# Down's column chunks taken in pairs with seven block products in two K pairs of each part, and token forms kept per K pair

## The chip, the core and the metric

The kernel runs on one core of a Trainium2 chip. The metric is the device time in microseconds (us) of one execution of the whole program. The median of three runs of the kernel before is 2602.59 us (2600.7 to 2604.3). Names of engines: TensorE (PE, and PEld for its weight loads), VectorE (DVE), ScalarE (ACT), GpSimd (POOL), and SyncE (SP), which issues the DMAs.

## The reference

A decoder trunk of two layers runs over 256 tokens of width 2048 in float32. Layer 0 has a state-space mixer, layer 1 differential attention, and each is followed by a SwiGLU FFN of width 5632. Every sub-layer has a norm ahead of it and one behind it:

```python
for i in range(DEPTH):
    h = rmsnorm(x, norm_mix_pre[i])
    m = ssd_mixer(h, ...) if i % 2 == 0 else diff_attention(h, ...)
    x = x + rmsnorm(m, norm_mix_post[i])
    h = rmsnorm(x, norm_ffn_pre[i])
    m = (silu(h @ ffn_w_gate[i]) * (h @ ffn_w_up[i])) @ ffn_w_down[i]
    x = x + rmsnorm(m, norm_ffn_post[i])
```

"Down" in this document is the product with `ffn_w_down` (5632 x 2048), "gate" and "up" those with the other two (2048 x 5632 each).

## The kernel before

**Products.** A float32 matrix product is made from two parts of each operand, hi (the value rounded to the type fp32r) and lo (the rest), as three matmuls: hi by hi, hi by lo, lo by hi. A matmul has a 128 x 128 block of activations as the stationary operand (128 rows of K, 128 tokens) and a 128 x 512 block of weights as the moving one. The 256 tokens are two halves, t = 0 and 1. A **K pair** is 256 rows of K (two blocks j), a **column chunk** is 512 output columns.

**Feeding.** Weights are loaded as 128 x 2048 tiles `raw` (1 MB) in a pool of three buffers; SP issues the loads in program order. `prep` (L112) then makes hi with a ScalarE cast (L119) and lo with a VectorE subtraction (L120), in a pool of four buffers each. If a split is late, TensorE waits. Weights that are split once serve both token halves.

**`mv` (L159)** is the plain product: for one column chunk it runs over K pairs. In each one it does t = 0 at once, puts t = 1 on the list `pending`, where it stays for `lag` K pairs, and calls `tick`. The two sums lie in PSUM (pool `accp`, four buffers), and `evac` is called for t when the last K pair of that t is done.

**`pair` (L201)** takes two column chunks at once, so that one K pair is a 2 x 2 x 2 product (token half, j, column chunk) of eight blocks, 24 matmuls. In the K pairs named by `SEVEN = (3, 5)` it takes seven block products, 21 matmuls, in the manner of Strassen and Winograd. That needs four sums of weight blocks (VectorE, L239 to L242), a second split of these sums, and four **token forms**, sums and differences of activation blocks, as stationary operands. Its order within such a K pair is: three products that need no sums of weights (p1, (0,0), (0,1), nine matmuls), a `tick`, then p6, p5, p7 and (1,0), which need the sums. p1, p5, p6, p7 are collected over both K pairs in their own PSUM tiles (pool `auxp`, four buffers, which the transposes of activations use as well). After the last seven-product K pair a ScalarE copy (L256) and four VectorE combinations (L257 to L260) make four tiles of them in SBUF, which `done` adds when a sum is complete. Gate and up of column chunks 0 to 9 go this way, the last chunk, 10, goes through `mv`.

**The FFN.** `ffn` (L699) runs gate and up in three parts of column chunks, (10, 0, 1), (2, 3, 4, 5), (6, 7, 8, 9), and behind each part does Down over the K pairs which that part has produced: 6, 8 and 8 K pairs. So Down of a part begins right behind the up pair that yields its last activations. `u_done` (L748) makes silu(gate) x up with two VectorE operations for each of four 128 x 512 pieces (L752, L753); `act_piece` transposes a piece on TensorE (L271) and splits it (L264, L265). The transposes are put off by two steps with `later(2, piece)`. `later`, `tick` and `lookup` are a list of deferred work: `tick` runs what is due, `lookup` runs it at once if something is needed.

**Down.** `out_proj` (L594) calls `mv` for n = 0 to 3, the four column chunks of the output, over the K pairs `kgs` of the part. The tiles m[(t, n)] hold the sum over parts: part one copies PSUM to them (L608), the others add (L610). In the last part, m[(t, n)] also enters the row's sum of squares, and is multiplied by the weights of the post-norm, `wpost`, one row of 512 columns that a DMA spreads over 128 partitions (L673). This product is made on GpSimd for n = 0, 1, 2 and on VectorE for n = 3 (L600). `load_post` keeps one n at a time in one buffer: when another n is asked for, it is loaded into the same buffer. After n = 3 follows `norm_chain` (L566), which completes the norm, adds the residual `x` and transposes it (`ptx`, L574) for the next sub-layer.

**Buffers for forms and for x.** `make_forms` (L717) makes the forms of a block of two K pairs, hence four token forms for each, though only one of the two K pairs is in `SEVEN`. It stores hi and lo in tiles with the tag `xr`, four buffers. The residual x, written to DRAM (`xr_d`) at the start of the FFN, is read back into tiles of the same tag by `fetch_x` (L688) ahead of the last part's Down.

**Order.** The program text gives dependencies; a scheduler then orders the instructions on each engine, as far as they allow. So the place of an instruction in an engine's queue isn't that of the text.

Of the kernel before, what the change touches and what calls it, by code (L numbers as in the profile page):

```python
# [30 lines left out]
LAG2 = 2  # L31

SEVEN = (3, 5)


@with_exitstack
def trunk_kernel(ctx, tc, x_rows, x_cols, vec_cols, vec64, post_rows, lam_rows,
# [110 lines left out]
    def lookup(dct, key):  # L148
        while key not in dct:
            deferred.popleft()[1]()  # L150
        return dct[key]
# [46 lines left out]
                    evac(ct, acc[ct][:, :S], acc[ct][:, S:])  # L198
            tick()

    def pair(blocks, seven, form, done):  # L201

        flush()
        acc = {}  # L210
        end = len(blocks) - 1

        def mm(k, st, hi, lo, last):
            first = k not in acc
            if first:
                acc[k] = (auxp.tile([P, 512], F32, tag="aux", name="cp") if isinstance(k, str) else
                          accp.tile([P, 512], F32, tag="acc", name="acc"))
            for q, (a, b) in enumerate(((st[0], hi), (st[0], lo), (st[1], hi))):
                nc.tensor.matmul(acc[k], a, b, start=first and q == 0, stop=last and q == 2)  # L219

        ss = {}
        for kp, src in enumerate(blocks):
            raw = rawp.tile([P, 4, 512], F32, tag="raw", name="raw")
            for c in range(2):
                nc.sync.dma_start(raw[:, 2 * c:2 * c + 2], src[c])
            if kp not in seven:
                hi, lo = prep(raw)
                for t in range(NT):
                    for c, e in ((0, 2), (1, 0)):
                        for j in range(2):  # L230
                            mm((t, c), x_stat(2 * kp + j, t), hi[:, e + j], lo[:, e + j], kp == end and j == 1)
                        if kp == end:
                            done(t, c, acc[(t, c)], ss)
                    tick()
                continue
            last = kp == seven[-1]
            hi, lo = prep(raw[:, 1:4])

            nc.vector.tensor_tensor(raw[:, 2], raw[:, 2], raw[:, 0], op=ALU.add)  # L239
            nc.vector.tensor_tensor(raw[:, 0], raw[:, 0], raw[:, 1], op=ALU.add)  # L240
            nc.vector.tensor_tensor(raw[:, 1], raw[:, 1], raw[:, 2], op=ALU.add)
            nc.vector.tensor_tensor(raw[:, 3], raw[:, 3], raw[:, 1], op=ALU.add)  # L242
            sh, sl = prep(raw)
            k0, k1 = 2 * kp, 2 * kp + 1
            mm("p1", x_stat(k0, 0), hi[:, 1], lo[:, 1], last)
            mm((0, 0), x_stat(k1, 0), hi[:, 2], lo[:, 2], False)
            mm((0, 1), form(kp, 3), hi[:, 0], lo[:, 0], False)
            tick()
            mm("p6", form(kp, 2), sh[:, 1], sl[:, 1], last)
            mm("p5", form(kp, 0), sh[:, 2], sl[:, 2], last)  # L250
            mm("p7", form(kp, 1), sh[:, 0], sl[:, 0], last)
            mm((1, 0), x_stat(k1, 1), sh[:, 3], sl[:, 3], False)
# [338 lines left out]
        if not final:  # L591
            later(2, stats)

    def out_proj(w, first, last, acts, kgs, step, final, lag, t512, pw, scale=None, ns=range(4)):  # L594

        def sums(t, n):
            mt = m[(t, n)]
            row_sumsq(ss4[t][:, n:n + 1], mt, t512("junk"))
            dst = t512("mw") if n == 3 else mt
            (nc.vector if n == 3 else nc.gpsimd).tensor_tensor(dst, mt, pw(n), op=ALU.mult)  # L600
            return dst

        ss4 = {}
        for n in ns:
            def evac(t, ps, n=n):
                if first:
                    m[(t, n)] = mpool.tile([P, 512], F32, tag="m", name="m")
                    nc.scalar.copy(m[(t, n)], ps)  # L608
                else:
                    nc.vector.tensor_tensor(m[(t, n)], m[(t, n)], ps, op=ALU.add)  # L610
                if not last:
                    return
                if t not in ss4:
                    ss4[t] = small.tile([P, 4], F32, tag="ss4", name="ss_m", bufs=3)
                    for e in range(n):
                        sums(t, e)
                dst = sums(t, n)
                if n == 2:
                    p3 = small.tile([P, 1], F32, tag="ss1", name="p3", bufs=3)
                    nc.vector.tensor_reduce(p3, ss4[t][:, 0:3], axis=AX.X, op=ALU.add)  # L620
                    nc.vector.tensor_scalar(ss4[t][:, 0:1], p3, 1.0 / D, EPS, op0=ALU.mult, op1=ALU.add)
                if n == 3:
                    norm_chain(t, ss4[t], dst, step, final, t512)

            def stat(i, j, t):
                hi, lo = lookup(acts, (t, kgs[i] // 2))
                jj = (kgs[i] % 2) * 2 + j
                return hi[:, jj], lo[:, jj]
# [49 lines left out]

    def xr_tile(name):
        return postp.tile([P, 2, 512], F32, tag="xr", name=name, bufs=4)

    def fetch_x(src):
        for t in range(NT):
            for h in range(2):
                xt = xr_tile("x")
# [14 lines left out]
    def ffn(wg, wu, wd, step, final):  # L702
# [14 lines left out]
        def make_forms(n):  # L717

            xf = []
            for t in range(NT):  # L720
                xf.append(t512("xf", (P, 4, P)))
                sl = slice(t * P, (t + 1) * P)
                nc.vector.tensor_tensor(xf[t], xT_hi[n][:, :, sl].bitcast(F32), xT_lo[n][:, :, sl].bitcast(F32), op=ALU.add)
            fa, fb = (t512("f", (P, 2, 2, P)) for _ in range(2))
            nc.vector.tensor_tensor(fa[:, 0], xf[1][:, 0:4:2], xf[1][:, 1:4:2], op=ALU.subtract)
            nc.vector.tensor_tensor(fa[:, 1], xf[1][:, 0:4:2], xf[0][:, 0:4:2], op=ALU.subtract)
            nc.vector.tensor_tensor(fb[:, 0], xf[0][:, 0:4:2], fa[:, 0], op=ALU.subtract)
            nc.vector.tensor_tensor(fb[:, 1], xf[0][:, 1:4:2], fb[:, 0], op=ALU.subtract)
            fh = postp.tile([P, 4, 2, P], F32R, tag="xr", name="fh", bufs=4)
            fl = postp.tile([P, 4, 2, P], F32R, tag="xr", name="fl", bufs=4)  # L730
            for k, f in enumerate((fa, fb)):
                split(fh[:, 2 * k:2 * k + 2], fl[:, 2 * k:2 * k + 2], f)
            forms[n] = (fh, fl)

        def form(kp, f):
            fh, fl = lookup(forms, kp // 2)
            return fh[:, f, kp % 2], fl[:, f, kp % 2]

        def g_done(p):
            def done(t, c, ps, ss):  # L740
# [27 lines left out]
        for k, n in enumerate(sorted({kp // 2 for kp in SEVEN})):  # L768
            later(1 + 3 * k, lambda n=n: make_forms(n))
        mv([wu[10, k] for k in range(4)], u_stat, u_evac, LAG2)  # L770
        parts = [(10, 0, 1), (2, 3, 4, 5), (6, 7, 8, 9)]
        for pi, part in enumerate(parts):
            for c in part:
                if c < 10 and c % 2 == 0:
                    pair(twos(wg, c), SEVEN, form, g_done(c // 2))
                    pair(twos(wu, c), SEVEN, form, u_done(c // 2))
            last = pi == len(parts) - 1
            if last:
                fetch_x(lambda t, h: xr_d[t][h].rearrange("p (e k) -> p e k", e=2))
            out_proj(wd, pi == 0, last, acts, [2 * c + e for c in part for e in range(2)], step, final, LAG2, t512,  # L780
                     load_post(step) if last else None)

    ffn(w_g0, w_u0, w_d0, 1, False)

# [183 lines left out]
```

## Time and profile before

| | |
|---|---|
| median of 3 runs | 2602.59 us (2600.7 to 2604.3) |
| profiled execution, its own time | 2600.35 us |
| its span in the profile | 2598.3 us |
| mean granted TensorE clock | 0.995 |
| data read from HBM | 483.71 MB, 189 GB/s over the span |
| chain that ended last: matmuls of `mv`, `pair`, `ws` (PE acc L168, L219, L193, L195) | 39%, 23%, 11%, 6% of the span |

The page of the profile gives busy time by engine, the chain of work that ended last, and the costliest groups of instructions. A row of the groups reads: line, engine, operation, output <- input, sizes, count, then busy time and the mean duration of one in ns, then the idle time just before them and what ended it. Matmuls overlap in the pipeline of TensorE, so their mean duration is longer than the distance from one to the next. The profiled execution is 2.05 us longer than its span, and 2.2 us shorter than the median.

### The profile page before, as it was taken

Reading aid. Unit: us, or ns where it says so; the run is one execution under the profiler, and the core shown is the slowest. Engines: PE = TensorE matmul, PEld = TensorE weight load, DVE = VectorE, ACT = ScalarE, POOL = GpSimd, SP = SyncE. Lnnn points to the kernel's source line nnn. Section 1 sums busy time; section 2 is a strip of 40 time slices with the busy share of each in tenths; the row PEclk is TensorE's granted clock in tenths of the full one; section 3 lists DMA queues with packets and bytes.
Section 4 is the critical chain, followed back from the end, with each engine's and each line's share of the span. In section 5 each row is a group of like instructions: output and inputs, shape, how many; then the busy total and the mean of one; then the engine's idle time right before and its main releaser. Section 6 shows DMA issues by size and latency. Waiting matters only on the chain.

```text
span 2598.3 us, 31297 instructions
## 1 busy us (share of the span) xinstructions
PE 2561.4 (99%) x12270; PEld 2105.6 (81%) x12270; DVE 1815.8 (70%) x2230; ACT 1276.9 (49%) x1506; POOL 158.4 (6%) x164
## 2 busy tenths in 40 slices
PE   8999999999999999999999999999999999999998
PEld 7878888888878888888888788887788888888886
DVE  7888757887687567846785666556577478657864
ACT  4555655555564444534453554445554444434442
POOL 2021000111100000000001100001100000000001
PEclk9999999999999999999999999999999999999999
DMA  6545554544754654655465544444555555555563
GB/s 223 189 142 201 183 194 174 194 167 162 267 214 163 222 199 162 220 187 202 168 243 203 189 145 167 174 157 144 212 188 207 179 203 189 203 181 191 198 231 137
DMA packets 111699, 492.10 MB, mean 189 GB/s; under 512 B 10880, under 2 KB 27584, under 8 KB 75712
## 3 DMA queue, kind: packets, MB, share of 16 engines
q1 hardware_dynamic: 110896, 489.27, 53.3%
q8 instruction: 96, 1.57, 0.2%
q10 hardware_dynamic: 656, 0.85, 0.1%
q14 instruction: 51, 0.42, 0.0%
HBM read 483.71 MB, written 6.36 MB: 189 GB/s over the span
## 4 chain that ended last, share of the span: by engine, by line
PE 86%; DVE 6%; issue 3%; ACT 2%; DMA 2%; POOL 0%; DVEq 0%; SPq 0%; ACTq 0%; POOLq 0%
PE acc L168 39%; PE acc L219 23%; PE acc L193 11%; PE acc L195 6%; PE cp L219 3%; DVE lo L120 2%; ACT hi L119 2%; PE sc L844 1%; DMA raw<-in_w_d_dram 1%; DMA raw<-in_w_g_dram 1%; PE py L498 1%; DVE v L423 1%; PE pt_f L271 1%; PE ptx L574 0%; PE pyt L508 0%
## 5 line engine op out<-in xcount | busy, mean ns | idle before, releaser
L120 DVE TENSOR_TENSOR lo<-raw,hi 128x2048 fp32r<-128x2048 f32 (+2 forms) x528 | 1030.4, 1961 | 609.2 <-ACT hi L119 608.8
L119 ACT CAST hi<-raw 128x2048 fp32r<-128x2048 f32 (+2 forms) x528 | 851.1, 1618 | 924.8 <-PE acc L168 250.4
L219 PE MATMUL acc<-hi,xT 128*128 128x512 f32 x2080 | 656.8, 390 | 0.0
L193 PE MATMUL acc<-xT,hi 128*128 128x512 f32 x1280 | 456.6, 401 | 0.0
L219 PEld LDWEIGHTS acc<-hi,xT 128*128 128x128 f32 x2080 | 390.5, 188 | 80.5
L219 PE MATMUL acc<-lo,xT 128*128 128x512 f32 x1040 | 405.0, 389 | 0.0
L195 PE MATMUL acc<-xT,lo 128*128 128x256 f32 x1280 | 359.7, 282 | 5.8 <-DVE lo L120 5.8
L168 PE MATMUL acc<-hi,xT 128*128 128x512 f32 x1024 | 334.9, 399 | 2.3 <-ACT xT L579 2.0
L193 PEld LDWEIGHTS acc<-xT,hi 128*128 128x128 f32 x1280 | 241.8, 189 | 57.1 <-issue 0.9
L168 PE MATMUL acc<-hi,ah_f 128*128 128x512 f32 x704 | 274.8, 390 | 0.0
L168 PE MATMUL acc<-lo,ah_f 128*128 128x512 f32 x704 | 274.6, 390 | 0.0
L168 PE MATMUL acc<-hi,al_f 128*128 128x512 f32 x704 | 273.8, 389 | 0.0
L195 PEld LDWEIGHTS acc<-xT,lo 128*128 128x128 f32 x1280 | 243.4, 190 | 8.3 <-DVE lo L120 6.7
L168 PEld LDWEIGHTS acc<-hi,xT 128*128 128x128 f32 x1024 | 191.8, 188 | 48.1 <-issue 5.1
L219 PEld LDWEIGHTS acc<-lo,xT 128*128 128x128 f32 x1040 | 195.3, 188 | 40.2
L168 PE MATMUL acc<-lo,xT 128*128 128x512 f32 x512 | 206.7, 404 | 1.6 <-DVE lo L120 1.6
L168 PEld LDWEIGHTS acc<-hi,ah_f 128*128 128x128 f32 x704 | 132.2, 188 | 27.3
L168 PEld LDWEIGHTS acc<-hi,al_f 128*128 128x128 f32 x704 | 132.2, 188 | 27.0
L168 PEld LDWEIGHTS acc<-lo,ah_f 128*128 128x128 f32 x704 | 132.2, 188 | 26.9
L600 POOL TENSOR_TENSOR m<-m,wpost 128x512 f32<-128x512 f32 x24 | 44.2, 1842 | 1462.8 <-ACT junk L282 1423.2
L124 DVE SCALAR_TENSOR_TENSOR lo<-raw,cols,hi 128x512 fp32r<-128x512 f32 x128 | 92.7, 771 | 52.0 <-ACT hi L123 51.7
L168 PEld LDWEIGHTS acc<-lo,xT 128*128 128x128 f32 x512 | 96.4, 188 | 23.7 <-issue 3.9
(251 smaller groups left out, 2701.0 us busy)
## 6 DMA issues: line engine op xcount, KB each, us to landing
raw<-in_w_d_dram SPq DMA_DIRECT2D x88, 1024.0 KB, 4.8
raw<-in_w_zxbc_dram SPq DMA_DIRECT2D x80, 1024.0 KB, 4.8
raw<-in_w_g_dram SPq DMA_DIRECT2D x160, 512.0 KB, 4.4
raw<-in_w_u_dram SPq DMA_DIRECT2D x160, 512.0 KB, 4.7
raw<-in_w_qkv_dram SPq DMA_DIRECT2D x48, 1024.0 KB, 4.7
raw<-in_w_so_dram SPq DMA_DIRECT2D x32, 1024.0 KB, 4.7
raw<-in_w_ao_dram SPq DMA_DIRECT2D x16, 1024.0 KB, 4.7
mt<-acum_d SPq DMA_DIRECT2D x16, 512.0 KB, 6.9
```

The lines of the kernel that those rows point to most:

```text
L119: nc.scalar.copy(hi, raw)
L120: nc.vector.tensor_tensor(lo, raw, hi.bitcast(F32), op=ALU.subtract)
L124: nc.vector.scalar_tensor_tensor(lo[:, j], raw[:, j], scale[j], hi[:, j].bitcast(F32), op0=ALU.mult, op1=ALU.subtract)
L168: nc.tensor.matmul(acc[t], a, b[:, j], start=(i == 0 and j == 0 and q == 0), stop=(i == last and j == 1 and q == 2))
L193: nc.tensor.matmul(acc[ct], hi[:, j, cs], x.rearrange("p a s -> p (a s)"), start=(i == 0 and j == 0), stop=False)
L195: nc.tensor.matmul(acc[ct][:, :S], lo[:, j, cs], x[:, 0], start=False, stop=(i == last and j == 1))
L219: nc.tensor.matmul(acc[k], a, b, start=first and q == 0, stop=last and q == 2)
L271: nc.tensor.transpose(pt[:, j], src[:, j * P:(j + 1) * P], ident)
L423: nc.vector.scalar_tensor_tensor(v, u[:, k:k + S], cwh[:, ch, k:k + 1], v, op0=ALU.mult, op1=ALU.add)
L498: nc.tensor.matmul(py[e * 64:(e + 1) * 64, a], xd[c][:, 2 * a + e], mts[c][:, 2 * a + e], start=True, stop=True)
L600: (nc.vector if n == 3 else nc.gpsimd).tensor_tensor(dst, mt, pw(n), op=ALU.mult)
L844: nc.tensor.matmul(sc[c][:, h], qT[cp, h, ts], kT[cp, h, :nk * P], start=True, stop=True)
```

## The change

Down goes through `pair` as well, with seven block products in two K pairs of each part: the second and the fourth of six in part one, the third and the sixth of eight in parts two and three (`DSEVEN`). Parts one and two take the output columns as pairs (0, 1) and (2, 3). Part three takes only (0, 1) as a pair, then reads x back, then does columns 2 and 3 with `mv` as before.

```diff
+DSEVEN = {6: (1, 3), 8: (2, 5)}

-    def pair(blocks, seven, form, done):
+    def pair(blocks, stat, seven, form, done):
...
-    def out_proj(w, first, last, acts, kgs, step, final, lag, t512, pw, scale=None, ns=range(4)):
+    def out_proj(w, first, last, acts, kgs, step, final, lag, t512, pw, scale=None, ns=range(4), two=()):
...
+        seven = DSEVEN[len(kgs)] if two else ()
+        for n in two:
+            def done(t, c, ps, ss, n=n):
+                y, op = ss[(t, c)]
+                k = (t, n + 1 - c)
+                if first:
+                    m[k] = mpool.tile([P, 512], F32, tag="m", name="m")
+                    nc.vector.tensor_tensor(m[k], ps, y, op=op)
+                else:
+                    nc.vector.tensor_tensor(y, ps, y, op=op)
+                    nc.vector.tensor_tensor(m[k], m[k], y, op=ALU.add)
+
+            if n == two[0]:
+                for i in seven:
+                    later(2 * i - 4, lambda i=i: make_form(forms, i, stat, "xrB", t512))
+            pair([[w[n + e, kg // 2][:, kg % 2 * 2:kg % 2 * 2 + 2] for e in range(2)] for kg in kgs],
+                 stat, seven, form, done)
```

The forms are made per K pair, for gate and up (tag `xrA`) as for Down (tag `xrB`), from sums hi + lo of four 128 x 128 blocks and four differences, then one split:

```diff
+    def make_form(dct, key, stat, tag, t512):
+        xf = t512("xf", (P, NT, 2, P))
+        f = t512("f", (P, 4, P))
+        for t in range(NT):
+            for j in range(2):
+                hi, lo = stat(key, j, t)
+                nc.vector.tensor_tensor(xf[:, t, j], hi.bitcast(F32), lo.bitcast(F32), op=ALU.add)
+        nc.vector.tensor_tensor(f[:, 0], xf[:, 1, 0], xf[:, 1, 1], op=ALU.subtract)
+        nc.vector.tensor_tensor(f[:, 1], xf[:, 1, 0], xf[:, 0, 0], op=ALU.subtract)
+        nc.vector.tensor_tensor(f[:, 2], xf[:, 0, 0], f[:, 0], op=ALU.subtract)
+        nc.vector.tensor_tensor(f[:, 3], xf[:, 0, 1], f[:, 2], op=ALU.subtract)
+        ff = xr_tile("ff", tag, (P, 4, 2, P), F32R)
+        split(ff[:, :, 0], ff[:, :, 1], f)
+        dct[key] = ff
...
-            if last:
-                fetch_x(lambda t, h: xr_d[t][h].rearrange("p (e k) -> p e k", e=2))
-            out_proj(wd, pi == 0, last, acts, [2 * c + e for c in part for e in range(2)], step, final, LAG2, t512,
-                     load_post(step) if last else None)
+            kgs = [2 * c + e for c in part for e in range(2)]
+            if not last:
+                out_proj(wd, pi == 0, False, acts, kgs, step, final, LAG2, t512, None, ns=(), two=(0, 2))
+                continue
+            out_proj(wd, False, False, acts, kgs, step, final, LAG2, t512, None, ns=(), two=(0,))
+            fetch_x(lambda t, h: xr_d[t][h].rearrange("p (e k) -> p e k", e=2))
+            out_proj(wd, False, True, acts, kgs, step, final, LAG2, t512, load_post(step), ns=range(2, 4))
```

The four buffers of the tag `xr` become two of `xrA` and two of `xrB`. In the last call, `sums` isn't reached for n = 0 and 1 as their sums become complete in the pair; the code that calls it is unchanged, and makes up for it when n = 2 and n = 3 are evacuated, token half by token half.

How the scheduler now orders the work is seen in three places. The first is VectorE's queue at the start of Down's part one in the first FFN. Before, the splits of Down's weights (`lo`) stand between the additions (L752) and products (L753) with which `u_done` ends the up pair, and the first split of transposed activations (`al_f`):

```order
L120 TENSOR_TENSOR lo_7653<-raw,hi_7652 128x2048
L120 TENSOR_TENSOR lo_7690<-raw,hi_7689 128x2048
L752 TENSOR_TENSOR s_7553<-acc,s_7553 128x512
L752 TENSOR_TENSOR sw<-acc,sw 128x512
L753 SCALAR_TENSOR_TENSOR s_7270<-s_7553,rs_pre_0_6681,s_7270 128x512
L753 SCALAR_TENSOR_TENSOR sw<-sw,rs_pre_0_6681 128x512
L752 TENSOR_TENSOR su<-acc,su 128x512
L120 TENSOR_TENSOR lo_7721<-raw,hi_7720 128x2048
```

In the change, the same place in the queue (`lo_7648` is the first K pair of Down, `lo_7727` the second, whose sums of weights are the rows L241 and L242 here and L243 and L244 further on):

```order
L122 TENSOR_TENSOR lo_7648<-raw,hi_7647 128x2048
L122 TENSOR_TENSOR lo_7727<-raw,hi_7726 128x1536
L241 TENSOR_TENSOR raw<-raw 128x512
L782 TENSOR_TENSOR s_7547<-acc,s_7547 128x512
L242 TENSOR_TENSOR raw<-raw 128x512
L783 SCALAR_TENSOR_TENSOR s_7264<-s_7547,rs_pre_0_6681,s_7264 128x512
L782 TENSOR_TENSOR sw<-acc,sw 128x512
L782 TENSOR_TENSOR su<-acc,su 128x512
```

```order
L720 TENSOR_TENSOR f<-xf 128x128
L266 TENSOR_TENSOR ff<-f,ff 128x4x128
L719 TENSOR_TENSOR f<-xf 128x128
L243 TENSOR_TENSOR raw<-raw 128x512
L721 TENSOR_TENSOR f<-xf,f 128x128
L244 TENSOR_TENSOR raw<-raw 128x512
L722 TENSOR_TENSOR f<-xf,f 128x128
L122 TENSOR_TENSOR lo_7735<-raw,hi_7734 128x2048
```

`lo_7735` is the split of the sums of the second K pair. Between the two pieces stand the rest of the gate products, four splits of activations and most of the two forms; the split of the sums comes behind all of these. The rows L719 to L722 of the second piece belong to the forms of the fourth K pair, and `ff` is the split of the second K pair's forms.

The second place is SP's queue at the end of the program. Before, a `wpost` is loaded after each n, among the loads of Down's weights:

```order
L109 DMA raw<-in_w_d_dram 128x2048 x8
L673 DMA wpost<-in_post_rows_dram 128x512
L109 DMA raw<-in_w_d_dram 128x2048 x4
L673 DMA wpost<-in_post_rows_dram 128x512
L109 DMA raw<-in_w_d_dram 128x2048 x2
L673 DMA wpost<-in_post_rows_dram 128x512
L570 DMA out_dram<-x 128x512 x8
```

In the change:

```order
L111 DMA raw<-in_w_d_dram 128x2048 x3
L700 DMA wpost<-in_post_rows_dram 128x512
L111 DMA raw<-in_w_d_dram 128x2048
L700 DMA wpost<-in_post_rows_dram 128x512
L111 DMA raw<-in_w_d_dram 128x2048 x3
L700 DMA wpost<-in_post_rows_dram 128x512 x4
L571 DMA out_dram<-x 128x512 x8
```

Four loads of `wpost` now stand together behind the last weights. An FFN has seven where it had four (24 instead of 18 in the program).

The third place is GpSimd's queue there: the six products with `wpost`, whose number names one load of it. Before, each load served two products, one of each token half:

```order
L600 TENSOR_TENSOR m_15904<-m_15904,wpost_19234 128x512
L600 TENSOR_TENSOR m_15943<-m_15943,wpost_19234 128x512
L600 TENSOR_TENSOR m_16000<-m_16000,wpost_19367 128x512
L600 TENSOR_TENSOR m_16039<-m_16039,wpost_19367 128x512
L600 TENSOR_TENSOR m_16096<-m_16096,wpost_19499 128x512
L600 TENSOR_TENSOR m_16135<-m_16135,wpost_19499 128x512
```

In the change, each product has a load of its own, n = 0, 1, 2 for half 0, then again for half 1:

```order
L604 TENSOR_TENSOR m_16294<-m_16294,wpost_19958 128x512
L604 TENSOR_TENSOR m_16286<-m_16286,wpost_19963 128x512
L604 TENSOR_TENSOR m_16515<-m_16515,wpost_19968 128x512
L604 TENSOR_TENSOR m_16310<-m_16310,wpost_20015 128x512
L604 TENSOR_TENSOR m_16302<-m_16302,wpost_20020 128x512
L604 TENSOR_TENSOR m_16531<-m_16531,wpost_20025 128x512
```

In counts: the program has 60 matmuls of 128 x 512 fewer; the loads of Down's weights are 160 instructions in place of 88 for the same bytes (two of 0.5 MB for a K pair in a `pair`), and DMAs issued by SP rise from 673 to 751 in all.

More of the change, by code (lines that the diff above doesn't have):

```diff
@@ L230, in pair @@
                         for j in range(2):
-                            mm((t, c), x_stat(2 * kp + j, t), hi[:, e + j], lo[:, e + j], kp == end and j == 1)
+                            mm((t, c), stat(kp, j, t), hi[:, e + j], lo[:, e + j], kp == end and j == 1)
                         if kp == end:
@@ L243, in pair @@
             sh, sl = prep(raw)
-            k0, k1 = 2 * kp, 2 * kp + 1
-            mm("p1", x_stat(k0, 0), hi[:, 1], lo[:, 1], last)
-            mm((0, 0), x_stat(k1, 0), hi[:, 2], lo[:, 2], False)
+            mm("p1", stat(kp, 0, 0), hi[:, 1], lo[:, 1], last)
+            mm((0, 0), stat(kp, 1, 0), hi[:, 2], lo[:, 2], False)
             mm((0, 1), form(kp, 3), hi[:, 0], lo[:, 0], False)
@@ L251, in pair @@
             mm("p7", form(kp, 1), sh[:, 0], sl[:, 0], last)
-            mm((1, 0), x_stat(k1, 1), sh[:, 3], sl[:, 3], False)
+            mm((1, 0), stat(kp, 1, 1), sh[:, 3], sl[:, 3], False)
             tick()
@@ L601, in sums, with stat, form @@
             return dst
+        def stat(i, j, t):
+            hi, lo = lookup(acts, (t, kgs[i] // 2))
+            jj = (kgs[i] % 2) * 2 + j
+            return hi[:, jj], lo[:, jj]
+        forms = {}
+        def form(i, f):
+            return form_of(lookup(forms, i), f)
+        seven = DSEVEN[len(kgs)] if two else ()
[14 more added lines that the diff above has]
+                 stat, seven, form, done)
         ss4 = {}
@@ L623, in evac @@
                     norm_chain(t, ss4[t], dst, step, final, t512)
[L625 to L628, printed above, removed]
             mv([w[n, kg // 2] for kg in kgs[::2]], stat, evac, lag,
@@ L677, in load_post, with xr_tile, form_of @@
         return get
-    def xr_tile(name):
-        return postp.tile([P, 2, 512], F32, tag="xr", name=name, bufs=4)
+    def xr_tile(name, tag, shape=(P, 2, 512), dtype=F32):
+        return postp.tile(list(shape), dtype, tag=tag, name=name, bufs=2)
+    def make_form(dct, key, stat, tag, t512):
[12 more added lines that the diff above has]
+        dct[key] = ff
+    def form_of(ff, f):
+        return ff[:, f, 0], ff[:, f, 1]
     def fetch_x(src):
@@ L686, in fetch_x @@
             for h in range(2):
-                xt = xr_tile("x")
+                xt = xr_tile("x", ("xrA", "xrB")[t])
                 nc.sync.dma_start(xt, src(t, h))
@@ L715, in u_evac, with kp_stat @@
             acts[(t, 10)] = act_piece(g, f"f{step}_10_{t}")
[L717 to L733, printed above, removed]
+        def kp_stat(kp, j, t):
+            return x_stat(2 * kp + j, t)
         def form(kp, f):
-            fh, fl = lookup(forms, kp // 2)
-            return fh[:, f, kp % 2], fl[:, f, kp % 2]
+            return form_of(lookup(forms, kp), f)
         def g_done(p):
@@ L767, in ffn @@
                 nc.sync.dma_start(xr_d[t][h].rearrange("p (e k) -> p e k", e=2), xr_of[(t, h)])
-        for k, n in enumerate(sorted({kp // 2 for kp in SEVEN})):
-            later(1 + 3 * k, lambda n=n: make_forms(n))
+        for k, kp in enumerate(SEVEN):
+            later(1 + 3 * k, lambda kp=kp: make_form(forms, kp, kp_stat, "xrA", t512))
         mv([wu[10, k] for k in range(4)], u_stat, u_evac, LAG2)
@@ L774, in ffn @@
                 if c < 10 and c % 2 == 0:
-                    pair(twos(wg, c), SEVEN, form, g_done(c // 2))
-                    pair(twos(wu, c), SEVEN, form, u_done(c // 2))
+                    pair(twos(wg, c), kp_stat, SEVEN, form, g_done(c // 2))
+                    pair(twos(wu, c), kp_stat, SEVEN, form, u_done(c // 2))
             last = pi == len(parts) - 1
-            if last:
-                fetch_x(lambda t, h: xr_d[t][h].rearrange("p (e k) -> p e k", e=2))
-            out_proj(wd, pi == 0, last, acts, [2 * c + e for c in part for e in range(2)], step, final, LAG2, t512,
-                     load_post(step) if last else None)
+            kgs = [2 * c + e for c in part for e in range(2)]
[5 more added lines that the diff above has]
+            out_proj(wd, False, True, acts, kgs, step, final, LAG2, t512, load_post(step), ns=range(2, 4))
     ffn(w_g0, w_u0, w_d0, 1, False)
```

## The prediction

> **What bounds the kernel now.** I read the page first, then the chain that ended last in order of time, then stretches of it.
>
> ```profile
> PE 2561.4 (99%) x12270; PEld 2105.6 (81%) x12270; DVE 1815.8 (70%) x2230; ACT 1276.9 (49%) x1506; POOL 158.4 (6%) x164
> ...
> PE 86%; DVE 6%; issue 3%; ACT 2%; DMA 2%; POOL 0%; DVEq 0%; SPq 0%; ACTq 0%; POOLq 0%
> ...
> 1104.30 83.43 PE acc L168 x368
> 1187.73 16.32 PE acc L219 x72
> ```
>
> TensorE is busy all the time and carries the chain. The last two rows are the chain's pieces in the second Down part of the first FFN and in the gate pair behind it: 83.43 / 368 and 16.32 / 72 both give 0.2267 us from one 512-column matmul to the next (the durations of 0.39 us on the page overlap). So a removed matmul is worth 0.2267 us, as long as nothing that feeds TensorE comes late. The next view, busy time by stretch, tells how much room the feeders have: first Down as it is (368 matmuls), then a stretch of gate/up pairs that already use seven products.
>
> ```profile
> 1104.30:1187.70 83.40, 83.40 (x369) 69.07 (x369) 40.62 (x25) 29.28 (x16) 0.00 (x0) 1.00 0.55 194
> 1278.30:1362.50 84.20, 84.19 (x379) 69.36 (x378) 66.16 (x59) 40.53 (x29) 0.00 (x0) 1.00 0.60 214
> ```
>
> The columns are length, then busy time of PE, PEld, DVE, ACT and POOL, clock, DMA. VectorE is busy 49% in Down and 79% in a pair. The pairs run without a stall, but with little left, and Down becomes such a stage.
>
> **What goes.** A seven-product step has 21 matmuls in place of 24. Each Down part has two such K pairs; parts one and two do both column pairs, part three only the first: 2 x (2 + 2 + 1) x 3 = 30 fewer per FFN, 60 in all, 60 x 0.2267 = **-13.6 us**. The token forms made ahead of gate/up halve, but that work lies beside matmuls, so it gains nothing. The halved weight DMAs (160 for 88) move the same bytes and are issued from an idle SP: 0.
>
> **The start of a Down part.** Here VectorE must finish the up pair (four additions, four gate products), split four transposed activations, make two token forms, add four weight blocks and split the sums. Before, there were plain splits only.
>
> ```profile
> L120 DVE TENSOR_TENSOR lo<-raw,hi 128x2048 fp32r<-128x2048 f32 x328 | 746.9, 2289 | 484.2 <-ACT hi L119 484.1
> L119 ACT CAST hi<-raw 128x2048 fp32r<-128x2048 f32 x328 | 624.7, 1912 | 689.8 <-PE acc L168 204.8 <-DVE raw L242 181.9 <-PE acc L193 84.6
> L120 DVE TENSOR_TENSOR lo<-raw,hi 128x1536 fp32r<-128x1536 f32 x40 | 70.2, 1754 | 52.9 <-ACT hi L119 52.8
> L265 DVE TENSOR_TENSOR al_f<-pt_f,ah_f 128x512 fp32r<-128x512 f32 x44 | 29.0, 681 | 4.1 <-ACT ah_f L264 4.1
> L239 DVE TENSOR_TENSOR raw<-raw 128x512 f32<-128x512 f32 x40 | 27.6, 691 | 1.3
> L727 DVE TENSOR_TENSOR f<-xf,f 128x256 f32<-128x256 f32 x4 | 1.7, 416 | 0.0
> ...
> 850.78 2.28 DVE L120 TENSOR_TENSOR lo<-raw,hi 128x2048 fp32r<-128x2048 f32 x1
> 853.89 2.29 DVE L120 TENSOR_TENSOR lo<-raw,hi 128x2048 fp32r<-128x2048 f32 x1 [0.83 <-ACT hi L119]
> 856.10 0.68 DVE L752 TENSOR_TENSOR s<-acc,s 128x512 f32<-128x512 f32 x1
> 856.70 0.68 DVE L752 TENSOR_TENSOR sw<-acc,sw 128x512 f32<-128x512 f32 x1
> 857.30 0.74 DVE L753 SCALAR_TENSOR_TENSOR s<-s,rs_pre,s 128x512 f32<-128x512 f32 x1
> 857.96 0.74 DVE L753 SCALAR_TENSOR_TENSOR sw<-sw,rs_pre 128x512 f32<-128x512 f32 x1
> ...
> 858.75 0.60 PE L271 MATMUL pt_f<-ident,s 128*128 128x128 f32 x4
> 859.18 0.60 PE L271 MATMUL pt_f<-ident,sw 128*128 128x128 f32 x4
> ```
>
> The groups give durations, the timeline gives the clock time of part one in the first FFN. In part one the seven-product pairs are the second and fourth of six. The second block's split, now 1536 wide, ends at 853.9 + 1.75 = 855.6. Between it and the split of the sums the new queue holds four additions of weights (0.70 each from start to start), four evacuations (0.62), four gate products (0.66), four activation splits (0.62), one split of forms (0.65) and 15 additions of 128x128. The trace has no such addition; 128x512 at 0.69 and 128x256 at 0.42 bound it by 0.14 and 0.42, and I take 0.25, on the line through both. Sum: 2.8 + 2.5 + 2.65 + 2.5 + 0.65 + 3.75 = 14.9, so the last weight addition ends at 870.5, ScalarE's cast of the sums at 872.4, the split at 874.7.
>
> TensorE ends the up pair at 858.75, does 16 transposes (1.7; it waits some 0.5 for one gate product), one plain K pair and the nine matmuls of the seven that need no sums: 33 x 0.2267 = 7.5, so it stands at 868.4. It waits 4.0 for the cast, does four, waits 1.4 for the split. The fourth pair repeats it more mildly: VectorE needs 0.65 + 2.2 + 1.75 + 2.9 to 882.1, cast 884.0, split 886.3; TensorE comes by 884.0 + 0.9, waits 1.4. With 0.7 for small waits in this part's second column pair (its VectorE list, 28.5 busy plus two waits of 2 for casts, is as long as TensorE's 138 x 0.2267 = 31.3) that is **8 us per FFN, 16 in all**; bounds 3 and 12 each, by the bounds of the small additions (2.1 to 6.3 in place of 3.75) and what the second half adds. In parts two and three the first seven is the third pair: 24 matmuls, 5.4 us, more cover, against the 5.4 waited. I put **0.75 each, 3 in all**, bounds 0 and 8.
>
> **The end of Down.** Columns 0 and 1 now finish together, so the weighting by the post-norm rows happens for n = 0, 1, 2 of token half 0, then again for half 1, and the one buffer of wpost is loaded seven times per FFN where it was four. Half 1's three multiplies on GpSimd each wait for a load that waits for the multiply before it; behind them the load for n = 3 waits, and VectorE's product with it stands ahead of everything that makes x.
>
> ```profile
> 1422.56 0.68 DVE L610 TENSOR_TENSOR m<-m,acc 128x512 f32<-128x512 f32 x1
> 1424.07 1.30 POOL L600 TENSOR_TENSOR m<-m,wpost 128x512 f32<-128x512 f32 x1 [11.17 <-ACT junk L282]
> 1431.23 2.29 DVE L120 TENSOR_TENSOR lo<-raw,hi 128x2048 fp32r<-128x2048 f32 x1 [1.30 <-ACT hi L119]
> 1431.89 2.77 POOL L600 TENSOR_TENSOR m<-m,wpost 128x512 f32<-128x512 f32 x1 [6.52 <-ACT junk L282]
> 1445.03 0.69 DVE L600 TENSOR_TENSOR mw<-m,wpost 128x512 f32<-128x512 f32 x1
> 1447.52 0.63 PE L574 MATMUL ptx<-ident,x 128*128 128x128 f32 x4 [0.64 <-issue]
> ...
> 684.55 1.32 POOL L600 TENSOR_TENSOR m<-m,wpost 128x512 f32<-128x512 f32 x1 [3.80 <-DMA wpost<-in_post_rows_dram]
> ...
> wpost<-in_post_rows_dram SPq DMA_DIRECT2D x1, 256.0 KB, 5.0
> ...
> wpost<-in_post_rows_dram SPq DMA_DIRECT2D x1, 256.0 KB, 3.3
> ```
>
> Call A the evacuation of n = 2, half 0 (1422.56 before). The multiply starts at A + 1.5, the product for n = 3 at A + 22.5. The two last rows are single loads: issued at 1391 beside weight loads it lands after 5.0 us, issued at 2574 with nothing beside it after 3.3; the step at 684.55 shows the same chain, at 3.8. A step is 1.3 + 0.05 + landing: 6.35 or 4.65. In FFN 0 weight loads of the attention run beside: three steps put the last multiply at A + 20.6, its end at 21.9, the load at 27.0, one multiply slowed like the one at 1431.89 (beside a VectorE split) makes 28.4. Late by 5.9; 0.64 + 0.3 of waits there are absorbed: **+5**, bounds 0 (all quiet) and 9. TensorE has nothing else in its queue there. At the end of FFN 1 only the first load has neighbours: 1.5 + 6.35 + 3 x 4.65 = A + 21.8, hidden with 0.7 spare; **+0.5**, bounds 0 and 6. [...]
>
> **A long stall costs twice.**
>
> ```profile
> 108.26 0.58 PE L195 MATMUL acc<-xT,lo 128*128 128x256 f32 x1 [2.87 <-DVE lo L120]
> ...
> 108.20:111.70 3.50, 3.44 (x11) 2.97 (x12) 3.50 (x5) 1.35 (x2) 0.00 (x0) 0.51 0.31 37
> ...
> 1458.00:1462.00 4.00, 2.62 (x12) 1.84 (x11) 3.56 (x7) 2.88 (x6) 0.03 (x1) 1.00 0.62 236
> ```
>
> After a wait of 2.87 the granted clock was 0.51 for the next 3.5 us; around one of 1.39 (third row) it stayed 1.00. So a stall over some 2.9 loses 1.7 more. In part one the next wait swallows it; at the end of FFN 0 it counts: **+1.7**, bounds 0 and 5. [...]
>
> **Sum:** -13.6 + 16 + 3 + 5 + 0.5 + 1.7 = +12.6. The profiled execution took 2600.35 (its span of 2598.3 and 2.05 around it); the median of the runs is 2.2 higher. 2600.35 + 12.6 + 2.2 = **2615 us**.
>
> **Rivals.** (1) *The feeders hold; faster.* If VectorE comes through the start of a part 4 us sooner, which takes additions of 128x128 near 0.14 and the weights' splits ahead of 850.78, TensorE never waits there, and with quiet loads only 2 us are given back: 2602.6 - 13.6 + 2 = 2591. For it: the gate/up pairs run at 79% VectorE without a stall. Against: they have three plain pairs ahead of the first seven and no forms in the queue; part one has one. 0.13. (2) *Half of it.* Part one loses 4 per FFN, the others 2, the loads land like the quiet row: -13.6 + 8 + 2 + 1 = 2600. 0.22. (3) *The chain of loads also shows at the very end*, when landings stay at 5.0: 1.5 + 4 x 6.35 = A + 26.9, plus a slowed multiply, +6: 2621. 0.10. (4) The forecast: 0.55. That fewer matmuls are removed than said is no rival: the instruction lists show 60 fewer.
>
> **Chances and range.** What a measurement can tell from no change is 0.2%, 5.2 us: faster is rival 1, same is rival 2, slower the forecast and rival 3. The forecast's own range is 2608 to 2630; to hold 8 in 10 it reaches down to include rival 2: 2595 to 2630.
>
> **What would show it.** TensorE's waits by releaser: some 4 us and 1.4 us for hi and lo of the second K pair in part one of each FFN, nothing above 1 us in parts two and three. GpSimd's timeline at the end of Down: six multiplies, the last three about 6 us apart in FFN 0, then ptx late by 5 with the clock at half behind it. Wrong is the forecast if VectorE's split of the sums in part one starts before 869, or if ptx comes less than 2 us late.

## The result, and the profile after

| | before | changed |
|---|---|---|
| median | 2601.64 us (2599.91 to 2604.3, 4 runs) | 2617.99 us (2610.79 to 2619.45, 4 runs) |
| ratio | | 1.0056, 95% interval 1.004 to 1.0072 |
| profiled execution, its span | 2600.35, 2598.3 | 2610.79, 2609.0 |

The change makes the kernel slower by 16.4 us; 2615 were predicted, 12.4 more than the median of before that was then on record (2602.59). The profiled execution is the fastest of the four, 10.7 us over that of before in its span.

The first view is the page: busy time by engine and the shares of the chain that ended last.

```profile
PE 2551.5 (98%) x12210; PEld 2095.1 (80%) x12210; DVE 1972.8 (76%) x2522; ACT 1303.9 (50%) x1528; POOL 159.1 (6%) x164
...
PE 85%; DVE 7%; ACT 3%; DMA 2%; issue 2%; POOL 1%; SPq 0%; DVEq 0%; ACTq 0%; POOLq 0%
```

TensorE has 60 matmuls fewer (12210 for 12270). VectorE has 157 us more of work, and its share of the chain rose, as did those of ScalarE and GpSimd. TensorE's waits by releaser (total, times, longest), first of the changed kernel, then of before, tell who is late:

```profile
PE ptx L575 <- DVE x L569: 8.6, 5, 7.0
...
PE cp L221 <- DVE lo L122: 4.8, 6, 1.3
PE cp L221 <- ACT hi L121: 4.8, 2, 2.4
...
PE pt_f L272 <- DVE sw L783: 0.9, 1, 0.9
```

```profile
PE ptx L574 <- DVE x L568: 1.7, 4, 0.6
...
PE pt_f L271 <- DVE su L753: 1.2, 3, 0.5
...
PE pt_f L271 <- DVE sx L753: 0.8, 3, 0.3
...
PE pt_f L271 <- DVE s L753: 0.6, 2, 0.3
```

The waits for hi and lo of the sums of weights (tile `cp`) are new, 2.4 us in each FFN for the cast, and the one for x at the end of the first FFN grew from 0.6 to 7.0. Something went, too: the transposes of activations wait 0.9 us in all, where they waited 2.6.

**The start of part one**, chain in order of time (start, length, what), first FFN:

```profile
866.26 0.61 DVE raw L244
...
866.95 1.91 ACT hi L121
...
868.88 2.30 DVE lo L122
...
871.23 2.93 PE cp L221 x6
```

The same place in the timeline, with the split of the form, the matmuls that use it, and the wait:

```profile
864.57 0.68 DVE L266 TENSOR_TENSOR ff<-f,ff 128x512 fp32r<-128x512 f32 x1
...
865.67 0.39 PE L221 MATMUL acc<-hi,ff 128*128 128x512 f32 x1
...
868.90 0.97 PE L221 MATMUL cp<-hi,ff 128*128 128x512 f32 x3 [2.39 <-ACT hi L121]
```

The last addition of weights (L244) stands at the end of VectorE's list there, the cast and the split follow, and TensorE, which had come to this place at 866.5, waits 2.4 and then 1.1. The form isn't late: its split ends at 865.25, and TensorE runs three matmuls with it from 865.67, ahead of the wait. The six matmuls behind it take 2.93 us, not 1.36 (six times 0.2267): the granted clock was 0.51 there, 0.98 in the 3.4 us before. Busy time by windows of 3.4 us (columns as in the prediction, the clock is third from the end), for part one of the first and of the second FFN:

```profile
867.90:871.30 3.40, 1.27 (x5) 0.75 (x5) 2.42 (x2) 3.40 (x4) 0.00 (x0) 0.98 0.00 0
871.30:874.70 3.40, 3.40 (x8) 2.71 (x9) 3.40 (x3) 1.24 (x1) 0.00 (x0) 0.51 0.66 180
874.70:878.10 3.40, 3.40 (x16) 2.79 (x15) 3.26 (x5) 0.00 (x0) 0.00 (x0) 1.00 0.86 287
...
2018.20:2021.60 3.40, 1.20 (x4) 0.67 (x4) 1.58 (x2) 3.40 (x3) 0.00 (x0) 0.98 0.00 0
2021.60:2025.00 3.40, 2.55 (x6) 2.06 (x7) 3.40 (x3) 2.17 (x2) 0.00 (x0) 0.50 0.43 104
2025.00:2028.40 3.40, 3.40 (x9) 2.63 (x9) 3.30 (x5) 0.00 (x0) 0.00 (x0) 0.51 1.03 322
```

The waits are the same in both FFNs (2.39 and 1.13 us), but the half clock lasts 3.41 us in the first (from 871.2) and 6.83 in the second (from 2021.5).

**The end of the first FFN** in the timeline: VectorE's evacuation of n = 2, half 0 (the moment A of the prediction), GpSimd's products with `wpost`, then the evacuation of n = 3, VectorE's product for it, and the first transpose of x:

```profile
1425.34 0.68 DVE L642 TENSOR_TENSOR m<-m,acc 128x512 f32<-128x512 f32 x1
...
1426.91 1.29 POOL L604 TENSOR_TENSOR m<-m,wpost 128x512 f32<-128x512 f32 x1 [12.97 <-ACT junk L283]
1431.65 1.65 POOL L604 TENSOR_TENSOR m<-m,wpost 128x512 f32<-128x512 f32 x1 [3.44 <-ACT hi L121]
1436.87 2.44 POOL L604 TENSOR_TENSOR m<-m,wpost 128x512 f32<-128x512 f32 x1 [3.57 <-DMA wpost<-in_post_rows_dram]
1444.43 1.30 POOL L604 TENSOR_TENSOR m<-m,wpost 128x512 f32<-128x512 f32 x1 [5.13 <-DMA wpost<-in_post_rows_dram]
...
1444.20 0.68 DVE L642 TENSOR_TENSOR m<-m,acc 128x512 f32<-128x512 f32 x1
1450.73 0.69 DVE L604 TENSOR_TENSOR mw<-m,wpost 128x512 f32<-128x512 f32 x1 [5.85 <-DMA wpost<-in_post_rows_dram]
...
1453.02 1.11 PE L575 MATMUL ptx<-ident,x 128*128 128x128 f32 x4 [6.95 <-DVE x L569]
```

Each product waits for the load that waits for the product before it. (For the second one the row names a cast, but its load was issued at 1428.23, when the first product had ended, and landed 3.25 later.) The end of the program shows the same chain with quiet loads (3.3 us from issue to landing), and its last product is late as well:

```profile
2591.70 0.69 DVE L642 TENSOR_TENSOR m<-m,acc 128x512 f32<-128x512 f32 x1 [7.36 <-PE acc L170]
2594.91 0.69 DVE L604 TENSOR_TENSOR mw<-m,wpost 128x512 f32<-128x512 f32 x1 [2.52 <-DMA wpost<-in_post_rows_dram]
```

The product could have started at 2592.4, when the sum was there. It starts 2.5 later, and the program's tail behind the last matmul is longer by as much.

### The profile page after: what moved, and what is told of

It is laid out like the page before. It is cut to its first block, busy times and chain, and to the rows that moved or that the text cites. A ratio compares the mean times of both kernels' runs of the same rounds, so it can differ in the third digit from the quotient of the medians.

```text
span 2609.0 us, 31718 instructions
## 1 busy us (share of the span) xinstructions
PE 2551.5 (98%) x12210; PEld 2095.1 (80%) x12210; DVE 1972.8 (76%) x2522; ACT 1303.9 (50%) x1528; POOL 159.1 (6%) x164
## 4 chain that ended last, share of the span: by engine, by line
PE 85%; DVE 7%; ACT 3%; DMA 2%; issue 2%; POOL 1%; SPq 0%; DVEq 0%; ACTq 0%; POOLq 0%
PE acc L221 34%; PE acc L170 25%; PE acc L195 11%; PE acc L197 6%; PE cp L221 5%; ACT hi L121 2%; DVE lo L122 2%; DMA raw<-in_w_d_dram 1%; PE sc L877 1%; PE py L499 1%; DVE v L424 1%; PE pt_f L272 1%; PE ptx L575 1%; DMA wpost<-in_post_rows_dram 1%; DVE raw L244 0%
## 5 line engine op out<-in xcount | busy, mean ns | idle before, releaser
L122 DVE TENSOR_TENSOR lo<-raw,hi 128x2048 fp32r<-128x2048 f32 (+2 forms) x548 | 1064.1, 1955 | 464.5 <-ACT hi L121 463.8
L121 ACT CAST hi<-raw 128x2048 fp32r<-128x2048 f32 (+2 forms) x548 | 877.3, 1613 | 903.0 <-DVE raw L244 284.8
L221 PE MATMUL acc<-lo,ah_f 128*128 128x512 f32 x456 | 178.5, 391 | 0.0
L221 PE MATMUL acc<-hi,al_f 128*128 128x512 f32 x456 | 177.9, 390 | 0.0
L221 PE MATMUL acc<-hi,ah_f 128*128 128x512 f32 x456 | 176.3, 395 | 1.2 <-ACT hi L121 1.2
L221 PE MATMUL cp<-hi,ff 128*128 128x512 f32 x360 | 122.4, 394 | 4.8 <-ACT hi L121 4.8
L125 ACT ACTIVATE hi<-raw,cols 128x512 fp32r<-128x512 f32 x128 | 84.5, 715 | 55.8 <-PE acc L170 39.3
L221 PEld LDWEIGHTS acc<-hi,ah_f 128*128 128x128 f32 x456 | 86.3, 189 | 20.5 <-ACT hi L121 2.8
```

The lines of the kernel that those rows point to most:

```text
L121: nc.scalar.copy(hi, raw)
L122: nc.vector.tensor_tensor(lo, raw, hi.bitcast(F32), op=ALU.subtract)
L125: nc.scalar.activation(hi[:, j], raw[:, j], AF.Copy, scale=scale[j])
```

## Experiments

The theory to be tested: (A) the starts of Down lose because VectorE's queue there is too long; (B) the ends lose because `wpost` is reloaded in a chain; the half clock adds to both. The rivals: the loads of weights or the making of forms is late; x is late for another reason; VectorE is short of time in all of Down. The time of each run is a median of 4 to 11 executions; kernels of one group ran on the same chip beside the kernel before. Before's own median differs by up to 1.8 us between groups (2600.47 to 2602.25), and a difference across groups is no more exact than that.

**The first group** (before: 2601.63). The changed kernel again, and each cause undone alone and with the other.

> The changed kernel once more. Its four executions so far lay at 2610.8 (the one with the trace) and 2617 to 2619, with granted clocks of 0.993 and 0.989 to 0.991. Theory: the place of the waits is fixed by the order on VectorE, and what differs is how often the clock drops behind a wait of 2.4 to 3 us. Then the median is again 2612 to 2620, and a trace of an execution near 2617 shows the same waits (2.4 and 1.1 in part one, 7 at the end of the first FFN) and one or more further stretches at half clock. Rival: the executions differ in the landing of DMAs; then the waits themselves differ by several us.

2613.44 us, ratio 1.0047 (1.0034 to 1.0061). The five executions lie at 2612.6 to 2615.7. The trace, of one at 2615.5, has the same waits as the first (2.4 for the cast, 6.9 for x), and other stretches of half clock: twice 3.41 us in part one of the first FFN, once in the second, twice at the end of the first FFN. So the waits are fixed and the half clock is not, as the theory has it. In all, this trace has half clock for eleven times 3.41 us and the first had it for eight times (what lies behind the last matmul not counted). Three more, at up to 1.7 us each (an estimate, half of 3.41), make up to 5.1, and the two executions are 4.7 apart. Six of the eleven lie ahead of the first FFN, where the change does nothing; there the first trace has two, and that of before five. So the first trace was lucky in this, and it may be the same with the three of the first four executions that reached 2617 to 2619: their granted clock was 0.989 to 0.991, that of the fastest 0.993, and 0.003 of 2615 us is, as an estimate, up to 8 us. They left no trace, so this isn't shown.

```diff
         ss4 = {}
+        if last and ns[0] == 2:
+            for t in range(NT):
+                ss4[t] = small.tile([P, 4], F32, tag="ss4", name="ss_m", bufs=3)
+            for e in range(2):
+                for t in range(NT):
+                    sums(t, e)
         for n in ns:
```

> The weighting of n = 0 and n = 1 is done for both token halves right behind the column pair, so that wpost is loaded four times per FFN as before the change, and no load waits between the last products. Theory (chain of wpost loads): the wait of 7.0 for ptx at the end of the first FFN falls to under 1, the half clock behind it goes, and the tail of the program shrinks by 2.5; in all 9 to 11 us less than the changed kernel, about 2608. Rival (the end is late for another reason, the order of x or of n = 3 on VectorE): ptx still waits 4 or more, and the time falls by less than 4.

2603.85 us, 9.6 less than the changed kernel in `again`, ratio to before 1.0009 (1.0 to 1.0017). No wait for ptx is over 0.6, and no half clock is left at the end of the first FFN. (B) holds.

```diff
-DSEVEN = {6: (1, 3), 8: (2, 5)}
+DSEVEN = {6: (2, 4), 8: (2, 5)}
```

> In part one the seven products are taken in the third and fifth of six K pairs, not in the second and fourth; all else as in the changed kernel. Theory (VectorE's queue at the start of Down): one more plain K pair gives TensorE 24 matmuls, 5.4 us, which covers the waits of 2.4 and 1.1; with the half clock behind them 4 to 5 us per FFN go, 8 to 10 in all, about 2609. Rival (VectorE is short for the whole part, not only at its start): the waits move to the later K pairs, with 1 to 2 us each, and at most 4 us go.

2604.17 us, 9.3 less, ratio 1.0009 (1.0 to 1.0018). The waits of 2.4 and 1.1 and the half clock are gone; 0.5, 0.8 and 1.2 are left (counted beyond the 0.2267 from one matmul to the next). (A) holds for the place. It doesn't yet tell what in the queue is too long.

> Both edits together. If the two losses are apart from each other, their gains add: 17 to 20 us less than the changed kernel, 2598 to 2601, 0.1 to 0.2% faster than before the change. If they overlap (one wait takes the place of the other), 2604 or more.

2595.81 us, 17.6 less; 9.6 and 9.3 make 18.9, so the losses are nearly apart from each other. Ratio to before 0.9979 (0.997 to 0.9988): with both causes weakened, the seven products pay.

**The second group** (before: 2600.47) asked what is too long, and what the places are worth.

```diff
+        eng = nc.gpsimd if tag == "xrB" else nc.vector
...
-                nc.vector.tensor_tensor(xf[:, t, j], hi.bitcast(F32), lo.bitcast(F32), op=ALU.add)
+                eng.tensor_tensor(xf[:, t, j], hi.bitcast(F32), lo.bitcast(F32), op=ALU.add)
```

(and so for the four differences)

> post_early (2603.9), with the eight sums and differences of each form of Down made on GpSimd in place of VectorE; the seven products stand in the second and fourth K pair of part one as in the change. Theory (VectorE's queue ahead of the additions of weights): some 14 additions of 0.2 us, about 3 us, go from ahead of the last weight addition, so the wait for the cast falls from 2.4 to under 0.5, and with the half clock behind it 3 to 5 per FFN go, 2594 to 2598. Rival (the forms themselves are what is late, or GpSimd and VectorE slow each other): TensorE waits for ff or for the same cast, and the time is 2602 or more.

2624.09 us, 20.2 more than post_early: a miss, and the rival's outcome. The wait for the cast did shrink to 1.3, but another one came. In part two of the first FFN (timeline):

```profile
1107.25 0.45 POOL L729 TENSOR_TENSOR f<-xf,f 128x128 f32<-128x128 f32 x1
1107.74 0.62 ACT L265 CAST ff<-f 128x512 fp32r<-128x512 f32 x1 [8.30 <-POOL f L729]
1108.26 1.55 ACT L265 CAST ah_f<-pt_f 128x512 fp32r<-128x512 f32 x3
1108.87 0.69 DVE L266 TENSOR_TENSOR al_f<-pt_f,ah_f 128x512 fp32r<-128x512 f32 x1 [2.78 <-ACT ah_f L265]
1109.48 0.74 DVE L790 SCALAR_TENSOR_TENSOR sx<-sx,rs_pre 128x512 f32<-128x512 f32 x1
...
1110.28 1.12 PE L272 MATMUL pt_f<-ident,sx 128*128 128x128 f32 x4 [3.60 <-DVE sx L790]
```

The form is late on GpSimd (four additions xf took 4.03 us there, 0.89 on VectorE). ScalarE's cast of it (`ff`) waits, three casts of activations stand behind that cast, VectorE's split behind those, the gate product sx behind the split, and TensorE's transposes wait 3.6 for sx. Nothing is said by it against (A): the work left VectorE, and the wait went through three other queues. The same edit in late_post:

> late_post with Down's sums and differences for the forms on GpSimd. In late_post three waits of 0.5 to 1.2 are left in part one of each FFN, on ScalarE's casts that follow VectorE's additions. Theory: with less on VectorE half of them go, 1 to 3 us less than late_post, 2593 to 2595. Rival: VectorE isn't what they wait for; no change within 1 us.

2622.0 us, a miss of the same kind: waits for sx of up to 3.6 in all the later parts. In part one of its first FFN the additions of weights end at 870.6, but ScalarE's cast of the sums starts only at 876.8, behind its cast of a form that GpSimd ends at 876.2; so waits of 2.4 and 1.8 are there which late_post doesn't have.

> post_early, but Down of part one goes through mv as before the change: 24 matmuls more than late_post (5.4 us), no seven-product steps at the start of Down. If part one with its seven products in the third and fifth K pair still loses in waits what they save (the trace of late_post has some 3 us of waits there per FFN), the time is within 2 us of late_post, 2594 to 2598, and below post_early by 6 or more. Rival (the seven products of part one pay once they stand late): 2600 or more.

Its edit: in part one, `out_proj` is called with the default `ns=range(4)` and without `two`. 2598.58 us, ratio 0.9992 (0.9983 to 1.0001). That is 5.3 below post_early though it has 24 matmuls more, 5.4 us; so at the place that the change chose, part one's seven products lost about twice what they saved. The comparison with late_post, 2.8 apart over two groups, lies between the two outcomes that were written down, and the intervals overlap: that part one, placed late, pays a little is a hint and not shown.

Against late_post:

```diff
-DSEVEN = {6: (2, 4), 8: (2, 5)}
+DSEVEN = {6: (2, 4), 8: (3, 6)}
```

> late_post with the seven products of parts two and three in the fourth and seventh of eight K pairs. Theory: what waits are left there (0.7 in part two, 0.7 and 0.8 in part three of the first FFN) are of the same kind, short cover ahead of the first seven, and go: 1 to 2 us less than late_post, 2594 to 2595. Rival (they come from VectorE's load in the middle): no change.

2593.21 us, ratio 0.9972 (0.9961 to 0.9982). The waits in parts two and three are gone from the trace; the gain of 2.6 on late_post is of the expected size, but the intervals of the two overlap.

**The third group** (before: 2602.25) shortened the queue without another engine.

```diff
+        made = {}
+
+        def stat1(i, j, t):
+            hi, lo = lookup(acts, (t, 10))
+            return hi[:, 2 + j], lo[:, 2 + j]
+
+        later(12, lambda: make_form(made, 1, stat1, "xrB", t512))
         parts = [(10, 0, 1), (2, 3, 4, 5), (6, 7, 8, 9)]
```

(`out_proj` takes `made` for part one, and makes only the form that isn't there)

> post_early (2603.9), with one form alone made earlier: that of the second K pair of part one, whose activations exist since column chunk 10, is made during the first gate pair, still on VectorE. Seven products in the second and fourth K pair as in the change. Theory (the length of VectorE's queue at the start of Down): eight additions of 0.2 and one split of 0.7, 2.3 us, go from ahead of the last weight addition; the wait of 2.4 for the cast falls below 0.5, and with part of the half clock behind it 1.5 to 4 per FFN go, 2596 to 2601. Rival (the additions of weights wait for a load or for PSUM, not for their place in the queue): the wait for the cast stays at 2 or more, 2603 or more.

2592.84 us, ratio 0.9964 (0.9952 to 0.9976): 11.0 below post_early, more than expected. Seven products stand where the change has them, and only nine small operations of VectorE (and one cast of ScalarE) were moved from the queue ahead of L244. What is left of the waits for `cp` and of those for casts:

```profile
PE acc L221 <- ACT hi L121: 2.6, 4, 1.0
...
PE cp L221 <- DVE lo L122: 2.3, 3, 1.6
...
PE cp L221 <- ACT hi L121: 0.4, 1, 0.4
```

The waits for `cp` in part one went altogether; those left are in parts two and three of the first FFN. Its timeline shows why the gain is larger than the 2.3 us taken out:

```profile
864.77 0.68 DVE L244 TENSOR_TENSOR raw<-raw 128x512 f32<-128x512 f32 x1
865.37 1.28 DVE L266 TENSOR_TENSOR al_f<-pt_f,ah_f 128x512 fp32r<-128x512 f32 x2
865.54 5.10 ACT L121 CAST hi<-raw 128x2048 fp32r<-128x2048 f32 x3
866.68 0.49 DVE L726 TENSOR_TENSOR xf<-ah_f,al_f 128x128 f32<-128x128 f32 x2
...
867.50 2.28 DVE L122 TENSOR_TENSOR lo<-raw,hi 128x2048 fp32r<-128x2048 f32 x1
...
867.53 0.39 PE L221 MATMUL cp<-hi,ah_f 128*128 128x512 f32 x1
```

The second form's small operations and two splits of activations now come behind L244, where ScalarE's cast hides them. The hi of the sums is there at 867.5 when TensorE comes to the first of the nine matmuls that don't even need it. With the waits all of the half clock behind them went. So (A) holds in the strong sense: not Down's load on VectorE as a whole, but what stands ahead of one addition.

The last two of this group are later versions of late36:

> late36 (2593.2), with the load of the attention's lambda rows and the four small VectorE operations on them moved behind the first v product of the attention. In late36 and late_post one of them stands ahead of the transposed x in VectorE's queue and waits 2.7 for its load, and TensorE 2.3 for x. Theory: that wait goes, and 2 to 3 us with it, 2590 to 2592. Rival: the start of the attention waits for something else that is as late; no change.

2593.61 us, ratio 0.9972 (0.9962 to 0.9981): a miss. TensorE's wait of 2.3 for VectorE's half of the transposed x went, and one of 1.5 for ScalarE's half of it came in its place.

> best, with the seven products of part one in the second and fifth K pair, the form of the second made early as in early_form. In late36 some 2.9 us per FFN are left as waits in part one (0.5, 0.8, 1.2, 0.4). Theory (VectorE's queue is short of room in the first column pair, and each operation taken out of it is worth its time): 1 to 3 us less than best, 2588 to 2591. Rival (the first seven at the second K pair still comes too soon): as best or up to 4 more.

2592.35 us, ratio 0.9965 (0.9953 to 0.9978). 1.3 less than best, within the scatter of both; no more than a hint.

**Alone** (before: 2600.78):

> early_form (2592.8) with the seven products of parts two and three in the fourth and seventh K pair, as in late36. In the trace of early_form 3.4 us of waits are left at the first seven of parts two and three of the first FFN (0.6; 0.5, 0.5 and 1.8). Theory (too little cover ahead of the first seven): they go, 1 to 3 us less, 2590 to 2592, the fastest version. Rival (late36 gained 2.6 on late_post only by scatter between executions): within 1 us of early_form.

2592.92 us, ratio 0.9968 (0.9956 to 0.998): no gain on early_form. That is the rival's outcome. The waits of parts two and three of the first FFN are gone from its trace, but others of 0.6 and 0.9 stand in part two of the second and right behind it, and the load of the attention's lambda rows costs it 2.4 (late36 2.3, early_form 0.7 at this place), with half clock behind it. So this doesn't tell the theory from the rival. The fastest versions (early_form, early36, best, best_early, late36) can't be told apart; all are 0.3 to 0.4% below the kernel before.

## Why the prediction held

The sum came out at +12.6 with its terms at -13.6, 16, 3, 5, 0.5 and 1.7; the two measurements of the changed kernel are 16.4 and 11.8 over before. By the prediction's steps:

- **What goes, -13.6: right.** Sixty matmuls are gone, and the distance stayed. early_form, which lacks the same sixty and has few waits, is 9.4 us faster than before (2602.25 - 2592.84). The other 4.2 are about its own balance of waits: 6.6 new ones (3.2 and 3.4, below), less 2.1 that its transposes of activations no longer wait (0.5 in place of 2.6). No run shows the 13.6 alone.
- **Part one, 16: right in place and size, and partly by errors that cancel.** early_form takes 11.0 out, and its trace still has 1.6 per FFN there (1.1 and 0.5): 14. The changed kernel's own trace comes to the same: 3.8 in each FFN for the two waits, 0.9 for the later ones, and 1.6 and 2.8 for the half clock. But the parts of the 8 (which add to 7.5 as written) were off. VectorE's list to the last weight addition took 13.8 us from the end of the second block's split, not 14.9 (an addition of 128x128 takes 0.2 from start to start, four in 0.89, where 0.25 was taken), and it began 0.9 earlier, measured from the end of TensorE's up pair, than was put. So the waits were 2.4 and 1.1 in place of 4.0 and 1.4, and the fourth K pair cost 0.4 and not 1.4. What filled the gap is the step "in part one the next wait swallows it" (the half clock): it failed. The clock is at half for 3.41 us in the first FFN, and for 6.83 in the second, and TensorE then starts a matmul every 0.43 us in place of 0.23, with little waiting to swallow it. The half clock also came after a wait of 2.4, though the estimate had it from 2.9.
- **Parts two and three, 3: right in sum.** The changed kernel's trace has 3.2 us there beyond the usual distance of matmuls (0.4 and 1.4 in part two; 0.6 and 0.8 in part three), and early_form's, in which these parts are as in the change, 3.4 (0.6; 0.5, 0.5 and 1.8), all in the first FFN. The pattern, 0.75 in each, was wrong, and so was "nothing above 1 us" (a wait of 1.3).
- **The chain of loads, 5 + 0.5 + 1.7: the mechanism was right, the terms too small.** post_early takes 9.6 out, 7.2 were estimated. In the first FFN the product for n = 3 is 5.8 late, 5.9 were worked out, but on two wrong numbers whose errors cancel by luck: it starts at A + 25.4, not A + 28.4 (steps of 4.7, 5.2 and 7.6 in place of three of 6.35), while its sum is there at A + 18.9, not A + 21.8, since VectorE evacuates n = 2 late, behind a split of weights. At the end of the program the same shift of A made the chain 2.5 late where 0.5 was put, though its loads landed after 3.3 us each: rival 3's place with less than half its price. The half clock at the wait of 7 lasted 10.24 us (from 1448.1), not the 3.5 of the estimate, but the wait itself fills the first 5.0; 5.3 us of it lie behind the wait and cost some 2.6 (an estimate, half of 5.3), where 1.7 was put.
- **Not in the sum:** the gate products come earlier in VectorE's queue than before, since fewer splits stand between them, and the transposes wait 1.7 us less in all.

The tests named beforehand came out thus: GpSimd's six products are there, the last three 5.2 and 7.6 apart where 6 was said. VectorE's split of the sums starts at 868.9, a hair before 869, the bound below which the forecast was to be wrong: by this sign, as written, it was wrong. Yet TensorE came 1.9 earlier than worked out (866.5 for 868.4), and so it waited all the same; ptx is 6 us later than the 0.6 before, not less than 2. A bound on a clock time was the poorer test: only the distance to TensorE's arrival decides.

## What to carry to other kernels

When work is taken off the engine that is full and put on the one that feeds it, look at the places where the two hand over after a change of stage: a mean load of 76% hides that moving nine small operations away from ahead of one addition brought 11 us here, and turned a kernel 0.1% slower than before into one 0.36% faster. A buffer that one owner reuses in a new order (here row by row for each half, in place of both halves for each row) becomes a chain of loads; restoring the order brought 9.6 us without any buffer more. And moving small work to an idle engine cost 20 us here, though it shortened the wait that it was meant to shorten, since the queues of three other engines came to wait for its result.

## What the hardware showed beside that

In the changed kernel's trace the stretches at half clock ahead of the program's tail last 3.41 us (at 137.3, 434.3 and 871.2), 6.83 (at 2021.5) and 10.24 (at 1448.1). The wait ahead of those at 871.2 and 2021.5 is the same, 2.39 us, and it cost 1.6 us of half clock in one FFN and 2.8 in the other. So here the length of a wait alone doesn't tell what follows it. In the trace of before, a wait of 2.87 was followed by a granted clock of 0.51 for 3.5 us, and around one of 1.39 the clock stayed at 1.00; in the changed kernel 2.39 was enough, where the prediction had some 2.9. What decides it is not shown.

In the trace of pool_forms GpSimd took 0.45 us and more for a subtraction of two 128x128 tiles, and 1.0 for each of the four sums of hi and lo above (4.03 us for the four), which VectorE does at 0.2 from start to start (0.89 for the four).
